# Seven-product MLPs: the order of block sums, evictions and splits, and the place of the token scale

## The chip, the cores and the metric

The kernel runs on one core of one Trainium2 chip. The metric is the device time of one execution in microseconds; one execution was also taken by the hardware profiler, and all rows below are of that one.

## What is computed

Four layers over 512 tokens of 1024 features: sparse attention, a gated convolution, a gated linear recurrence, a gated linear attention. Behind each of the first two stands an MLP, which the change is about:

```python
def rmsnorm(x, g):
    y = xf * lax.rsqrt(jnp.mean(xf * xf, axis=-1, keepdims=True) + EPS)
    return (y * g.astype(jnp.float32)).astype(x.dtype)

def sq_relu_mlp(h, w1, w2):                     # w1 1024x4096, w2 4096x1024
    return jnp.square(jax.nn.relu(h @ w1)) @ w2
...
        h = h + sq_relu_mlp(rmsnorm(h, norm_mlp_g[i]), mlp_w1[i], mlp_w2[i])
    return rmsnorm(h, final_g)                  # then the third layer, which begins with rmsnorm_2
```

## The kernel before, in words

Activations lie features by tokens, `h` as eight tiles of 128x512. Every matrix product is done three times, with both operands split into a rounded high part and a remainder: `whi`, `wlo` for weights, `XH`, `XL` for inputs, `UH`, `UL` for hidden features. Weights come as 512 KB chunks of 128x1024 in one fixed stream (`wall`), issued on SyncE's queue by `dma_to` (L114) into four `stg` buffers, or into named blocks. `split_to` (L121) makes `whi` on ScalarE (L130) and `wlo` on VectorE (L131); both go into a ring of three pairs, and every fourth split of an MLP into a pair of its own (`mine`), for which the splitting runs three items ahead instead of two (`next_weights`). The order on each engine is the order of the code; there is no scheduler.

`chunk` multiplies one weight chunk with eight input tiles: 24 matmuls of 128x512. Outputs take one of three PSUM banks ("mm"), which a later output may use when the earlier one has been read.

`mlp` (from L590) runs eight groups of 512 hidden features. Each of the first seven has a feature stage of four chunks (m = 0 to 3) and a product stage of seven products. A group's part of `h @ w1` goes through relu (L611) and square (L612) on ScalarE into `raw`. The second matrix product is done on halves of tokens and features with seven products in place of eight: the left operands are sums of token halves of `raw` (`left`, L623 and L627 to L629, VectorE; `parts` splits them, L616 on ScalarE and L617 on GpSimd), the right operands are the blocks B11, B21, B22 of `w2` and the sums T3, T2, T4, T1 of blocks (`right`, L638 to L644, VectorE; T1 is written over B12). The products run in the order of `PRODUCTS`: B11, T3, B21, T2, T4, T1, B22. Each has two output tiles of six matmuls (L694 to L696), and but for T1 and B22, which stay in PSUM over all groups, VectorE adds each tile to a sum in SBUF (`sums`, L703; ScalarE copies in the first group, L701). These additions are the evictions spoken of here.

The norm's scale of a token is applied late: relu then square makes it the square of the scale, which is held per token as `cols` and, spread over partitions, as `rs2`. In the seventh group's end the sums are combined (`gather`), scaled by `cols` and transposed back onto `h` (L720, L722). The eighth group is plain: its features `u` are split whole (L671, L672), and eight outputs of 12 matmuls are multiplied by `rs2` (L759) and added to `h` (L760). Behind each output `after` splits `h` for the next layer (`operand`: XH on ScalarE, XL on VectorE, L283) and adds its square to `sacc` (`add_sq`: square on ScalarE, addition on GpSimd, L291). In the second MLP (`halves`) the sum of squares for its own norm is made inside its first group, at m = 1 and 2, and its `after_last` sums squares twice, into `sacc` and, scaled by `final_g`, into `sacc2`. The layer behind it begins with chunks xa0, xa1, xa2 on the unscaled input; `comb_a` turns both sums into scales `rc` and `r2` behind xa1 and `comb_b` spreads them by TensorE behind xa2. `softplus_neg`, 27 small VectorE instructions, is issued between xa0 and xa1.

## Time and profile before

| | us |
|---|---|
| median of 3 runs | 1885.51 (1884.52 to 1885.54) |
| the profiled execution's own time | 1884.3 |
| its span, first to last instruction | 1882.5 |
| TensorE busy | 1780.7 |
| mean granted clock of TensorE | 0.976 |

A granted clock of 1.00 is TensorE's full rate. In a timeline a row gives start, duration, engine, line, instruction and, in brackets, the idle time ahead of it and what ended it; "x2" merges two neighbours. The rows come below.

### The profile page before, as it was taken

Reading aid. Unit: us, or ns where it says so; the run is one execution under the profiler, and the core shown is the slowest. Engines: PE = TensorE matmul, PEld = TensorE weight load, DVE = VectorE, ACT = ScalarE, POOL = GpSimd, SP = SyncE. Lnnn points to the kernel's source line nnn. Section 1 sums busy time; section 2 is a strip of 40 time slices with the busy share of each in tenths; the row PEclk is TensorE's granted clock in tenths of the full one; section 3 lists DMA queues with packets and bytes.
Section 4 is the critical chain, followed back from the end, with each engine's and each line's share of the span. In section 5 each row is a group of like instructions: output and inputs, shape, how many; then the busy total and the mean of one; then the engine's idle time right before and its main releaser. Section 6 shows DMA issues by size and latency. Waiting matters only on the chain.

```text
span 1882.5 us, 22829 instructions
## 1 busy us (share of the span) xinstructions
PE 1780.7 (95%) x8712; PEld 1482.2 (79%) x8712; DVE 1214.9 (65%) x1688; ACT 934.0 (50%) x1424; POOL 503.9 (27%) x408
## 2 busy tenths in 40 slices
PE   9999999988898999898988898989999999999998
PEld 7887787777777778897777777778888788988887
DVE  5896455666667757756666676697676753565354
ACT  5334545444344534556444444557766654356553
POOL 1433311211112202436121112151231200662230
PEclk9999999999999999999999999999999999999999
DMA  5221114322221123103322231222222232232121
GB/s 184 79 90 57 57 63 150 101 90 89 79 101 45 57 88 112 45 24 124 101 79 79 93 98 55 82 97 81 99 95 85 90 101 90 90 107 68 52 72 46
DMA packets 45934, 159.71 MB, mean 85 GB/s; under 512 B 5217, under 2 KB 6625, under 8 KB 45824
## 3 DMA queue, kind: packets, MB, share of 16 engines
q1 hardware_dynamic: 45824, 158.24, 25.4%
q8 instruction: 69, 1.13, 0.2%
q14 instruction: 41, 0.34, 0.1%
HBM read 156.13 MB, written 2.10 MB: 84 GB/s over the span
## 4 chain that ended last, share of the span: by engine, by line
PE 73%; DVE 14%; ACT 7%; issue 5%; POOL 1%; DMA 0%; SPq 0%; DVEq 0%; ACTq 0%; POOLq 0%
PE w L177 4%; PE w L178 4%; PE w L176 4%; DVE wlo L131 3%; PE w L694 3%; PE w L695 3%; PE w L696 3%; ACT whi L130 2%; PE ko L177 1%; PE ko L176 1%; PE ko L178 1%; PE a L176 1%; PE a L177 1%; PE a L178 1%; DVE raw L629 1%
## 5 line engine op out<-in xcount | busy, mean ns | idle before, releaser
L131 DVE TENSOR_TENSOR wlo<-stg,whi 128x1024 fp32r<-128x1024 f32 x191 | 248.4, 1305 | 139.4 <-ACT whi L130 138.1
L130 ACT ACTIVATE whi<-stg 128x1024 fp32r<-128x1024 f32 x228 | 239.1, 1053 | 148.8 <-PE w L695 40.5
L617 POOL TENSOR_TENSOR UL<-raw,UH 128x512 fp32r<-128x512 f32 (+1 forms) x84 | 130.9, 1558 | 475.9 <-ACT UH L616 430.2
L176 PE MATMUL w<-XH,whi 128*128 128x512 f32 (+1 forms) x520 | 202.2, 389 | 0.0
L178 PE MATMUL w<-XH,wlo 128*128 128x512 f32 (+1 forms) x520 | 201.6, 388 | 0.0
L177 PE MATMUL w<-XL,whi 128*128 128x512 f32 (+1 forms) x520 | 201.4, 387 | 0.0
L694 PE MATMUL w<-whi,UH 128*128 128x512 f32 x280 | 120.5, 430 | 54.7 <-DVE sB L703 47.2
L695 PE MATMUL w<-whi,UL 128*128 128x512 f32 x280 | 117.1, 418 | 4.4 <-POOL UL L617 4.4
L131 POOL TENSOR_TENSOR wlo<-stg,whi 128x1024 fp32r<-128x1024 f32 x37 | 89.2, 2417 | 109.9 <-ACT whi L130 109.8
L694 PEld LDWEIGHTS w<-whi,UH 128*128 128x128 f32 x280 | 57.4, 205 | 75.2 <-DVE sB L703 52.4
L696 PE MATMUL w<-wlo,UH 128*128 128x512 f32 x280 | 116.3, 415 | 0.0
L291 POOL TENSOR_TENSOR sacc<-sacc,sq 128x512 f32<-128x512 f32 (+1 forms) x57 | 75.4, 1331 | 147.0 <-ACT sq L290 82.9
L178 PEld LDWEIGHTS w<-XH,wlo 128*128 128x128 f32 x520 | 97.7, 188 | 20.6
L177 PEld LDWEIGHTS w<-XL,whi 128*128 128x128 f32 x520 | 97.7, 188 | 20.3
L176 PEld LDWEIGHTS w<-XH,whi 128*128 128x128 f32 x520 | 97.7, 188 | 20.1
L611 ACT ACTIVATE relu<-w 128x512 f32<-128x512 f32 x64 | 38.1, 595 | 140.8 <-PE w L178 139.8
L616 ACT ACTIVATE UH<-raw 128x512 fp32r<-128x512 f32 (+1 forms) x84 | 59.1, 704 | 81.2 <-DVE raw L629 60.5
L131 DVE TENSOR_TENSOR wlo<-B,whi 128x1024 fp32r<-128x1024 f32 x56 | 76.3, 1365 | 27.1 <-ACT whi L130 27.1
L130 ACT ACTIVATE whi<-B 128x1024 fp32r<-128x1024 f32 x56 | 58.9, 1052 | 68.8 <-PE w L695 68.8
L176 PE MATMUL ko<-XH,whi 128*128 128x256 f32 x256 | 75.5, 295 | 2.4 <-ACT XH L977 2.4
L177 PE MATMUL ko<-XL,whi 128*128 128x256 f32 x256 | 74.5, 291 | 2.3 <-DVE XL L979 1.6
L178 PE MATMUL ko<-XH,wlo 128*128 128x256 f32 x256 | 74.1, 290 | 0.0
(528 smaller groups left out, 4860.7 us busy)
## 6 DMA issues: line engine op xcount, KB each, us to landing
stg<-wall SPq DMA_DIRECT2D x228, 512.0 KB, 3.3
B<-wall SPq DMA_DIRECT2D x56, 512.0 KB, 3.5
gst<-gwall SPq DMA_DIRECT2D x4, 512.0 KB, 3.8
h<-xT SPq DMA_DIRECT2D x3, 512.0 KB, 5.9
out<-yo SPq DMA_DIRECT2D x6, 256.0 KB, 2.5
stg<-wall SPq DMA_DIRECT2D x8, 128.0 KB, 4.8
h<-xT SPq DMA_DIRECT2D x2, 256.0 KB, 3.9
ex<-wglr SPq DMA_DIRECT2D x2, 256.0 KB, 2.7
```

What stands on the lines that cost most here:

```text
L130: act.activation(hi, src, AF.Copy)
L131: eng.tensor_tensor(out=lo, in0=src, in1=hi, op=ALU.subtract)
L176: pe.matmul(o, lhsT=hi[:, w], rhs=xh[:, k, ns], start=first, stop=False)
L177: pe.matmul(o, lhsT=hi[:, w], rhs=xl[:, k, ns], start=False, stop=False)
L178: pe.matmul(o, lhsT=lo[:, w], rhs=xh[:, k, ns], start=False, stop=last)
L291: eng.tensor_tensor(out=acc, in0=acc, in1=t, op=ALU.add)
L611: act.activation(r, o, AF.Relu)
L616: act.activation(UH[:, j, u0:u1, :], raw[:, r0:r1, :], AF.Copy)
L617: pool.tensor_tensor(out=UL[:, j, u0:u1, :], in0=raw[:, r0:r1, :], in1=UH[:, j, u0:u1, :], op=ALU.subtract)
L694: pe.matmul(o, lhsT=UH[:, j, i, xs], rhs=hi[:, js], start=s0, stop=False)
L695: pe.matmul(o, lhsT=UL[:, j, i, xs], rhs=hi[:, js], start=False, stop=False)
L696: pe.matmul(o, lhsT=UH[:, j, i, xs], rhs=lo[:, js], start=False, stop=s1)
```

## The change

Four things. In the groups, each sum of weight blocks is issued one chunk earlier, and the last three left parts (4 to 6 of the second half) are split behind the first product's evictions rather than in the feature stage; splits that run three items ahead are issued behind a product's evictions rather than ahead of its matmuls. In the plain group the token scale is multiplied into `u` and no longer into the outputs, and the transposes of `gather` come one chunk later. In the second MLP, the additions of squares for its norm go from GpSimd to VectorE, two a chunk. And the scaled sum of squares `sacc2` is made on VectorE behind xa0 instead of on GpSimd in `after_last`.

```diff
 # left
-                    parts(j, raw, 4, 7, 5)
+                    if j == 0:
+                        parts(j, raw, 4, 7, 5)
 # right
                 if m == 0:
                     for n in ("T2", "T3", "T4"):
                         f[n] = mp.tile([P, 1024], F32, tag=n, name=n, bufs=1)
+                    dve.tensor_tensor(out=f["T3"], in0=f["B22"], in1=f["B12"], op=ALU.subtract)
                 elif m == 1:
-                    dve.tensor_tensor(out=f["T3"], in0=f["B22"], in1=f["B12"], op=ALU.subtract)
-                elif m == 2:
                     dve.tensor_tensor(out=f["T2"], in0=f["T3"], in1=f["B11"], op=ALU.add)
                     dve.tensor_tensor(out=f["T4"], in0=f["T2"], in1=f["B21"], op=ALU.subtract)
-                else:
+                elif m == 2:
                     f["T1"] = f["B12"]
                     dve.tensor_tensor(out=f["T1"], in0=f["B12"], in1=f["B11"], op=ALU.subtract)
 # groups
-                    if halves and g == 0 and m in (1, 2):
-                        for q in range(4 * m - 4, 4 * m):
-                            add_sq(q, h[:, q, :], sacc)
+                    if halves and g == 0:
+                        for q in (2 * m, 2 * m + 1):
+                            add_sq(q, h[:, q, :], sacc, eng=dve)
...
                         hidden(m, o, u.rearrange("p (a b) -> p a b", a=2))
+                        dve.tensor_tensor(out=u, in0=u, in1=rs2, op=ALU.mult)
...
-                for n, i in PRODUCTS:
-                    hi, lo = next_weights()
+                for p, (n, i) in enumerate(PRODUCTS):
+                    hi, lo = weights(2)
...
                             dve.tensor_tensor(out=a, in0=o, in1=a, op=ALU.add)
+                    if p == 0:
+                        parts(1, raw, 4, 7, 5)
+                    if any(mine(cur[0] + q) for q in range(3)):
+                        split_to(cur[0] + 2)
 # gather
+                        elif m == 2:
                             back("T4", 1, 0)
-                        elif m == 2:
                             back("T3", 1, 4)
+                        else:
                             back("T2", 0, 4)
-                        else:
                             back("B11", 0, 0)
 # outputs of the plain group
-                t = tmp("y")
-                dve.tensor_tensor(out=t, in0=o, in1=rs2, op=ALU.mult)
-                dve.tensor_tensor(out=h[:, m, :], in0=h[:, m, :], in1=t, op=ALU.add)
+                dve.tensor_tensor(out=h[:, m, :], in0=o, in1=h[:, m, :], op=ALU.add)
 # after_last
-        add_sq(m, h[:, m, :], sacc2, scale=V("gfin", m))
 # do_xa, behind the matmuls of xa0
             if m == 0:
+                for q in range(KD):
+                    add_sq(q, h[:, q, :], sacc2, scale=V("gfin", q), eng=dve)
                 softplus_neg()
```

VectorE, third group of the first MLP, end of the feature stage and first evictions (sB11, sT3 are the sums, the numbers are buffers), before:

```order
L131 TENSOR_TENSOR wlo_3246<-B21_2997,whi_3245 128x1024
L627 TENSOR_TENSOR raw_3235<-raw_3235 128x256
L628 TENSOR_TENSOR raw_3235<-raw_3235 128x256
L629 TENSOR_TENSOR raw_3235<-raw_3235 128x256
L644 TENSOR_TENSOR B12_3043<-B12_3043,B11_2995 128x1024
L131 TENSOR_TENSOR wlo_3289<-T2_3161,whi_3288 128x1024
L703 TENSOR_TENSOR sB11_2474<-w2_3292,sB11_2474 128x512
L703 TENSOR_TENSOR sB11_2474<-w2_3300,sB11_2474 128x512
L703 TENSOR_TENSOR sT3_2475<-w2_3308,sT3_2475 128x512
L703 TENSOR_TENSOR sT3_2475<-w2_3316,sT3_2475 128x512
```

The same place now:

```order
L644 TENSOR_TENSOR B12_3059<-B12_3059,B11_2995 128x1024
L131 TENSOR_TENSOR wlo_3247<-B21_2997,whi_3246 128x1024
L627 TENSOR_TENSOR raw_3237<-raw_3237 128x256
L628 TENSOR_TENSOR raw_3237<-raw_3237 128x256
L629 TENSOR_TENSOR raw_3237<-raw_3237 128x256
L704 TENSOR_TENSOR sB11_2474<-w2_3282,sB11_2474 128x512
L704 TENSOR_TENSOR sB11_2474<-w2_3290,sB11_2474 128x512
L131 TENSOR_TENSOR wlo_3305<-T2_3161,whi_3304 128x1024
L704 TENSOR_TENSOR sT3_2475<-w2_3308,sT3_2475 128x512
L704 TENSOR_TENSOR sT3_2475<-w2_3316,sT3_2475 128x512
```

The sum T1 (written to B12) went from behind the three feature sums to ahead of the split, and the split of T2 from ahead of the evictions of sB11 to behind them.

VectorE behind the second MLP, from the last XL of the next layer's input to the first steps of `softplus_neg` (de, s1); before:

```order
L283 SCALAR_TENSOR_TENSOR XL_79<-h_77,gfe_6903,XH_78 128x512 x2
L131 TENSOR_TENSOR wlo_9564<-stg_9376,whi_9563 128x1024
L1071 TENSOR_SCALAR de_9595<-ex_9593 128x16
L1072 RECIPROCAL de_9595<-de_9595 128x16
L1074 TENSOR_TENSOR s1_9598<-ex_9593,de_9595 128x16
```

The same place now:

```order
L283 SCALAR_TENSOR_TENSOR XL_79<-h_77,gfe_6891,XH_78 128x512 x2
L131 TENSOR_TENSOR wlo_9518<-stg_9363,whi_9517 128x1024
L291 TENSOR_TENSOR sacc2_122<-sacc2_122,sq_9546 128x512
L291 TENSOR_TENSOR sacc2_122<-sacc2_122,sq_9549 128x512
L291 TENSOR_TENSOR sacc2_122<-sacc2_122,sq_9552 128x512
L291 TENSOR_TENSOR sacc2_122<-sacc2_122,sq_9555 128x512
L291 TENSOR_TENSOR sacc2_122<-sacc2_122,sq_9558 128x512
L291 TENSOR_TENSOR sacc2_122<-sacc2_122,sq_9561 128x512
L291 TENSOR_TENSOR sacc2_122<-sacc2_122,sq_9564 128x512
L1073 TENSOR_SCALAR de_9571<-ex_9569 128x16
L1074 RECIPROCAL de_9571<-de_9571 128x16
```

Seven additions into sacc2 came in between the split of a chunk and the first step of softplus.

## Rows read from the trace of the kernel before

**Rows 1.** The page: busy time, share of the span, instructions of each engine.

```profile
PE 1780.7 (95%) x8712; PEld 1482.2 (79%) x8712; DVE 1214.9 (65%) x1688; ACT 934.0 (50%) x1424; POOL 503.9 (27%) x408
```

**Rows 2.** TensorE's waits, whole span: releaser: us in total, times, longest.

```profile
PE w L694 <- DVE sB L703: 47.2, 12, 5.5
PE xa L177 <- DVE XL L283: 5.9, 2, 3.5
PE w L695 <- POOL UL L617: 4.4, 1, 4.4
PE w L694 <- DVE sT L703: 3.6, 4, 0.9
PE a L177 <- DVE XL L283: 3.1, 3, 2.0
...
PE w L694 <- ACT sB L701: 2.9, 1, 2.9
```

**Rows 3.** Timeline of TensorE's matmuls, first MLP, third group: start, duration in us.

```profile
392.05 0.39 PE L695 MATMUL w<-whi,UL 128*128 128x512 f32 x1
392.28 0.39 PE L696 MATMUL w<-wlo,UH 128*128 128x512 f32 x1
398.14 0.80 PE L694 MATMUL w<-whi,UH 128*128 128x512 f32 x1 [5.47 <-DVE sB L703]
...
403.42 0.50 PE L694 MATMUL w<-whi,UH 128*128 128x512 f32 x1
```

**Rows 4.** Stretches: busy us by engine (instructions), granted clock, DMA share, GB/s.

```profile
304.20:314.20 10.00, 9.99 (x36) 8.00 (x37) 4.09 (x4) 6.38 (x10) 0.00 (x0) 0.83 0.38 127
350.00:360.00 10.00, 9.09 (x38) 7.16 (x39) 9.39 (x12) 4.19 (x5) 1.06 (x1) 1.00 0.57 187
...
398.00:403.00 5.00, 4.86 (x12) 3.81 (x12) 3.17 (x6) 1.06 (x1) 0.00 (x0) 0.50 0.21 84
...
658.60:668.60 10.00, 7.23 (x26) 5.30 (x26) 6.94 (x6) 5.07 (x7) 3.53 (x7) 0.83 0.49 142
...
1242.00:1252.00 10.00, 7.57 (x21) 5.30 (x22) 8.86 (x16) 4.67 (x8) 5.84 (x4) 0.66 0.27 74
```

**Rows 5.** Timeline of VectorE, the same group.

```profile
387.89 2.20 DVE L641 TENSOR_TENSOR T<-T,B 128x1024 f32<-128x1024 f32 x1
390.02 1.21 DVE L131 TENSOR_TENSOR wlo<-B,whi 128x1024 fp32r<-128x1024 f32 x1
391.15 1.51 DVE L627 TENSOR_TENSOR raw<-raw 128x256 f32<-128x256 f32 x1
...
395.44 2.04 DVE L131 TENSOR_TENSOR wlo<-T,whi 128x1024 fp32r<-128x1024 f32 x1 [0.72 <-ACT whi L130]
397.40 1.27 DVE L703 TENSOR_TENSOR sB<-w,sB 128x512 f32<-128x512 f32 x2
```

**Rows 6.** Timeline of ScalarE and of GpSimd, the same group.

```profile
388.56 0.60 ACT L611 ACTIVATE relu<-w 128x512 f32<-128x512 f32 x1 [0.23 <-PE w L178]
...
394.59 1.81 POOL L617 TENSOR_TENSOR UL<-raw,UH 128x768 fp32r<-128x768 f32 x1 [2.21 <-issue]
```

**Rows 7.** Timeline of GpSimd and VectorE, the group ahead of it.

```profile
349.23 1.83 POOL L617 TENSOR_TENSOR UL<-raw,UH 128x768 fp32r<-128x768 f32 x1 [1.29 <-issue]
...
349.28 1.27 DVE L703 TENSOR_TENSOR sB<-w,sB 128x512 f32<-128x512 f32 x2
```

**Rows 8.** Timeline of GpSimd, second MLP, first group.

```profile
870.88 7.29 POOL L291 TENSOR_TENSOR sacc<-sacc,sq 128x512 f32<-128x512 f32 x4
```

**Rows 9.** Timeline of VectorE, plain group of the first MLP.

```profile
657.16 0.69 DVE L760 TENSOR_TENSOR h<-h,y 128x512 f32<-128x512 f32 x1
```

**Rows 10.** Timeline of VectorE, then of TensorE, behind the second MLP.

```profile
1250.01 0.18 DVE L1071 TENSOR_SCALAR de<-ex 128x16 f32<-128x16 f32 x1 [0.80 <-ACT ex L1069]
...
1260.31 0.16 DVE L1098 TENSOR_TENSOR r<-r,rc 128x4 f32<-128x4 f32 x1
...
1261.81 0.60 PE L303 MATMUL spread<-ident,r 128*128 128x128 f32 x4
```

## The prediction

> **What bounds the kernel now.** The page comes first: TensorE is busy 95% of the span and no other engine over 65% [rows 1], so the time is TensorE's own work plus whatever makes it wait or run slowly. Second the table of TensorE's waits [rows 2]: almost all of its idle time lies in the two MLPs, and one row leads: 47.2 us in twelve waits for a VectorE eviction of a product sum (sB). Six rows that this change touches come to 47.2 + 5.9 + 4.4 + 3.6 + 3.1 + 2.9 = 67.1 us. Third the timeline of one such wait [rows 3]: a 128x512 matmul follows the next after 0.23 us ahead of it, then comes a gap of 5.47 us, and from 398.14 to 403.42 there are twelve steps of 0.44 us. The granted clock of that stretch is 0.50 [rows 4], the 1.2 GHz level in place of 2.4, so a long wait is paid twice. Fourth the granted clock in the ten microseconds from the end of each wait [rows 4]: 1.00 after waits of about 1.3 us, 0.83 after one of 2.9 us, 0.66 at the worst place. Twelve such windows lose clock (first and last shown), together 27.3 us; I take 27, since a little of it lies in idle time counted already. The ceiling for this change is 67.1 + 27 = 94.1 us.
>
> **Where the long wait comes from.** It is one of order. The matmul output has three banks, so with the third tile of products done (392.5) TensorE needs the first eviction. VectorE reaches it at 397.40 [rows 5], because ahead of it in its queue stand, from 387.89 on: sum T4 (2.20), a split (1.21), three feature sums (1.51 and two of 0.42), sum T1 (1.21, the split's form) and the split of T2 (2.04). The 0.42 is what is left: 391.15 to the idle time ahead of 395.44 are 3.57, less 1.51 and 1.21, for two. Two of these are long only because VectorE stood behind GpSimd: a split takes 1.21 at 390.02 and 2.04 at 395.44, where GpSimd's 1.81 us subtraction began first [rows 5, 6].
>
> **Sums one chunk earlier, evictions ahead of splits.** No instruction is added here; T3, T2/T4 and T1 move to the chunk before, and the last three feature parts (ScalarE copy, GpSimd subtraction) and the split of T2 go behind the first product's two evictions. In the trace's group of 388 us the new queue reads so: T4 is done in the chunk before (VectorE is idle there; cover exists, one chunk is 24 x 0.23 = 5.5 us). Ahead of the eviction remain T1 1.21, one split 1.2 to 1.7, three feature sums 0.42 + 0.42 + 0.42 plus up to 1.0 for one GpSimd overlap. The feature sums can't start before ScalarE's relu and square, 388.56 + 0.6 + 0.6 = 389.8 [rows 6]. So the eviction starts between 391.1 (389.8 and three sums, nothing in the way) and 393.3 (all of it in the way), and frees its bank 0.75 later: TensorE waits between 0 and 1.5 us in place of 5.47. What is late next is the seventh tile, whose bank waits for the evictions of T3, and ahead of those VectorE now meets the moved split of T2, which waits for the moved GpSimd subtraction (1.81): about 1.0 more. I added the row durations queue by queue in this way for every group, with VectorE and GpSimd excluding each other where both read two SBUF tiles. Done on the old order, the six waits of one MLP for sB come to 24.3 us where the trace has 47.2 / 2 = 23.6, and that is my warrant for it. On the new order it leaves 1.4, 2.4, 1.5, 1.5, 1.5 and 2.4 us in the six groups behind the first, no single wait over 1.5. In the first group, whose evictions are ScalarE's, the 2.9 us wait goes. That is 10.7 us left per MLP, 21.4 in both. SP's queue: block loads are issued when the sum T1 or a split has read the old block; in the new order that is earlier or up to one product (2.8 us) later, while a block is next read a chunk or more after it lands.
>
> The Trainium skill, "SBUF — State Buffer", "Who interferes with whom", says that a VectorE instruction with two SBUF inputs and a GpSimd instruction that reads SBUF exclude each other for the whole instruction. This speaks against moving the subtraction to where the T2 split meets it. The trace agrees (2.04 against 1.21); had they merely shared bandwidth, the second wait of a group would be about 0.7 us shorter, some 8 us in all. The same section exempts an instruction with one SBUF input, and the evictions beside a GpSimd subtraction [rows 7], 1.27 for two, show that.
>
> **Squares of the second MLP's input to VectorE.** Seven GpSimd additions leave its queue in the first group, four of them in one run of 7.29 us [rows 8], behind which a feature part came late; the 4.4 us wait goes. VectorE gets seven of 0.69 [rows 9], two a chunk, beside 5.5 us of matmuls. My walk leaves 1.0 us at the first product's UL. Bounds 0 and 2.
>
> **Token scale into the last group's features.** At the end one of two VectorE instructions per output goes (about 0.7), the addition stays. Four multiplications (0.69, by the two-tile addition of [rows 9]) go in ahead of the feature copies, three hidden by 5.5 us chunks; the fourth delays the last feature part by 0.7, but the transposes that the gather now issues there (eight more) keep TensorE busy for 0.9, so nothing is added; uncovered it would be 0.7 per MLP. At the end VectorE's pair of outputs sinks by 1.4 us; the first chunk behind MLP 1 loses its 3.1 us waits and their slow matmuls, the first behind MLP 2 its 5.9 us, where GpSimd also loses eight additions. The gather moves transposes by one chunk; its own 1.5 us wait stays.
>
> **The second sum of squares, moved behind chunk xa0.** Here something is given back. Eight ScalarE squares and seven VectorE additions (0.69 by [rows 9], each needing the last: about 5.0) now stand ahead of the softplus chain and of the scale r. From the first step of that chain to r are 10.5 us in the trace (1250.01 to 1260.47), and r is done 1.3 us before TensorE asks for it with its transposes at 1261.81 [rows 10]. VectorE can begin the additions 4.5 us behind the start of xa0, when its last XL and a split are out, so they end at 9.6 and r comes at 20.1; TensorE, which no longer stalls in xa0, asks after three chunks and the means, 3 x 5.46 + 1.6 = 18.0. Bounds: 0, if softplus isn't blocked by GpSimd as it was in the trace, and 5, if the additions are; my walk has 2.0, and 1.4 for slow matmuls behind it. I take 3.4.
>
> **Sum.** 94.1 - 21.4 (groups) - 1.0 (first group) - 3.4 (r) - 1.5 (a slow matmul, 0.1, behind each small wait) = 66.8 us. The profiled execution took 1884.3 (span 1882.5, 1.8 around it): 1817.5. The median of the runs shown, 1885.5, is 1.2 higher, so I forecast 1819.
>
> **Rivals.** *Small waits hold the clock down.* A group has two or three waits of 0.4 to 1.5 us in 8 us. For it: behind three waits of 3.1 us together at the end of MLP 1 the clock fell to 0.83 [rows 4]. Against: two waits in a group of 350 us left 1.00 [rows 4]. If every one of the twelve groups loses 1.7 us (0.83 of 10 us), 20 us go: 1839. The Trainium skill, "TensorE: Matmul & The Clock Gate", "A second HAM failure mode: psum-queue depth-cycling", describes this: frequent micro-idles between matmul groups while output banks cycle make the clock oscillate. The waits after 350 us speak against it here, the sum of several for it.
>
> *The small waits vanish*, if the feature sums miss GpSimd each time: 22 us less, 1797.
>
> *The order reaches only half.* The eviction still stands behind the three feature sums; were these blocked by GpSimd twice, it comes at 395 and a 2.5 to 3 us wait with its 1.7 us of clock stays: 12 x 4.5 - 21 = 33 us more, 1852.
>
> *Slower: splits late.* VectorE now does two evictions (1.27) and then a split (1.21) for each product, 2.5 us against 12 x 0.23 = 2.76 of matmuls. If a product took VectorE over 2.76, TensorE would wait for a wlo at every one of 98 products; it eats up the whole gain of 67 when a product takes 0.7 more than that. With the split blocked as at 395.44 (2.04) and an eviction held up by half a microsecond in each product it would be 3.8: 98 x 1.0 - 67 = 31 us more than now, 1916. Against: GpSimd works in one product of seven.
>
> *Nothing changes*: if another wait of equal length stood behind the eviction. The queue lists show none.
>
> **How the numbers follow.** Forecast 0.60 (1806 to 1830 for errors of 0.5 us in each group's wait); clock held down 0.15 (1839); small waits vanish 0.10 (1797); half 0.07 (1852); slower 0.05; no change 0.03. The range 1800 to 1840 holds the first two and half of the third, 0.80. Faster by over 0.2% 0.92, within 0.2% 0.03, slower 0.05; 0.2% (3.8 us) is about what a measurement of this kernel can tell from no change.
>
> **What would show it.** Right: the sB row under 25 us and none over 1.6; no wait for UL or XL over 1.5 us; granted clock of the ten microseconds behind each group's waits near 1.00; a new wait of about 2 us of "spread" for r. Wrong: sB waits near 3 us; windows at 0.8 with short waits; wlo as a releaser of TensorE.

## The result, and the profile after

The changed kernel takes 1825.09 us (median of four runs, 1824.04 to 1827.32) against 1885.34: a ratio of 0.9683, 95% interval 0.9666 to 0.9700, or 60.3 us less. The forecast was 1819. The profiled execution has a span of 1825.6, at the upper end of its runs.

The page's line of busy times, which answers to [rows 1]:

```profile
PE 1764.9 (97%) x8712; PEld 1469.5 (80%) x8712; DVE 1205.7 (66%) x1694; ACT 932.4 (51%) x1424; POOL 480.3 (26%) x394
```

TensorE's waits over the whole span (line waited on, releaser, us in total, times, longest), which answer to [rows 2]:

```profile
PE w L695 <- DVE sT L704: 9.0, 10, 0.9
PE w L695 <- DVE sB L704: 5.6, 10, 1.4
PE w L696 <- POOL UL L617: 4.9, 6, 1.1
...
PE w L695 <- ACT UH L616: 3.4, 1, 3.4
PE yT L725 <- DVE sT L714: 2.6, 2, 1.3
...
PE spread L303 <- DVE r L1100: 2.0, 1, 2.0
```

The row of 47.2 us has become one of 5.6, and no wait in it is over 1.4. The waits for XL behind both MLPs are gone. Four things stand in the place: many short waits for sT and UL, one of 3.4 us for UH, and one of 2.0 for the scale r. The third group of the first MLP, TensorE and then VectorE, answers to [rows 3, 5]:

```profile
389.65 0.39 PE L697 MATMUL w<-wlo,UH 128*128 128x512 f32 x1
390.46 0.50 PE L695 MATMUL w<-whi,UH 128*128 128x512 f32 x1 [0.42 <-DVE sB L704]
...
394.41 0.50 PE L695 MATMUL w<-whi,UH 128*128 128x512 f32 x1 [0.90 <-DVE sT L704]
394.74 0.39 PE L696 MATMUL w<-whi,UL 128*128 128x512 f32 x1
394.97 0.40 PE L697 MATMUL w<-wlo,UH 128*128 128x512 f32 x1
```

```profile
387.48 0.41 DVE L627 TENSOR_TENSOR raw<-raw 128x256 f32<-128x256 f32 x1
387.93 1.42 DVE L628 TENSOR_TENSOR raw<-raw 128x256 f32<-128x256 f32 x1
389.38 0.42 DVE L629 TENSOR_TENSOR raw<-raw 128x256 f32<-128x256 f32 x1
389.72 1.28 DVE L704 TENSOR_TENSOR sB<-w,sB 128x512 f32<-128x512 f32 x2
391.66 2.09 DVE L131 TENSOR_TENSOR wlo<-T,whi 128x1024 fp32r<-128x1024 f32 x1 [0.66 <-ACT whi L130]
393.68 1.27 DVE L704 TENSOR_TENSOR sT<-w,sT 128x512 f32<-128x512 f32 x2
```

The eviction of sB now stands directly behind the feature sums, and TensorE waits 0.42 us for it in place of 5.47. The split of T2, which stood ahead of it, has become the next thing that is late: 2.09 us, with a wait of 0.90 behind it. Behind neither wait does the pace fall: steps of 0.23 us go on. The granted clock (the third number from the end, columns as in [rows 4]) of stretches with such waits, of the stretch behind the wait of 3.4 us, and of the one behind the wait of 2.0:

```profile
347.00:357.00 10.00, 9.06 (x40) 7.11 (x39) 9.47 (x11) 4.52 (x5) 1.54 (x1) 1.00 0.17 53
387.00:397.00 10.00, 8.68 (x37) 6.46 (x36) 9.27 (x12) 5.38 (x6) 3.14 (x2) 1.00 0.27 96
477.00:487.00 10.00, 9.63 (x42) 7.73 (x43) 10.00 (x13) 4.54 (x5) 1.42 (x1) 1.00 0.31 104
849.90:859.90 10.00, 9.11 (x29) 6.99 (x30) 8.10 (x8) 8.45 (x15) 4.87 (x3) 0.70 0.34 107
1203.00:1213.00 10.00, 9.85 (x41) 8.20 (x42) 9.09 (x13) 4.68 (x8) 0.00 (x0) 0.83 0.43 150
```

The waits of 0.25 to 1.39 us in the groups leave the full clock; the two longer ones do not. Length alone does not decide it: in ul_vector and t3_back (below) the same wait of 2.0 us for r leaves 1.00.

Lengths on TensorE, taken as differences of starts in the timelines (the seven groups of the first MLP, its plain group's features, its eight outputs; then the same for the second MLP's first group alone), in us:

| kernel | g1 | g2 | g3 | g4 | g5 | g6 | g7 | features | outputs | 2nd MLP g1 |
|---|---|---|---|---|---|---|---|---|---|---|
| before | 45.9 | 45.4 | 49.4 | 48.3 | 48.4 | 44.1 | 48.3 | 27.0 | 22.3 | 49.6 |
| changed | 42.8 | 44.3 | 44.1 | 42.8 | 42.9 | 43.0 | 44.1 | 26.9 | 22.4 | 48.5 |
| undo_sums | 41.5 | 44.2 | 44.2 | 43.4 | 47.8 | 43.0 | 45.8 | 26.9 | 22.4 | 46.6 |
| undo_parts | 44.1 | 44.2 | 44.1 | 42.8 | 48.2 | 43.0 | 44.1 | 26.9 | 22.4 | 48.7 |
| undo_splits | 42.4 | 45.4 | 44.1 | 42.8 | 45.6 | 44.1 | 44.0 | 26.9 | 22.4 | 47.9 |
| order_only | 42.7 | 44.3 | 44.1 | 42.8 | 42.9 | 43.0 | 44.1 | 25.4 | 21.6 | 51.3 |
| undo_scale | 42.5 | 44.3 | 44.1 | 42.8 | 42.9 | 43.0 | 44.1 | 25.4 | 21.6 | 47.4 |
| ul_vector | 44.8 | 43.1 | 43.0 | 41.7 | 42.9 | 41.8 | 43.0 | 26.9 | 22.4 | 47.6 |
| t3_back | 43.2 | 44.2 | 44.1 | 42.8 | 42.9 | 43.0 | 44.1 | 26.9 | 22.4 | 43.9 |

The first groups differ by up to 2.6 us also between kernels that are alike there (in the first MLP 42.2 to 44.8 for ul_vector, all_three and three_edits; in the second 47.4 to 49.9 for the changed kernel, undo_scale, undo_sacc2 and softplus_late); the others repeat to 0.1 us. By stage, before to changed: first MLP 379.1 to 353.4, the convolution behind it 197.2 to 194.4, second MLP 383.0 to 359.1, from there to the spread of r 27.3 to 20.5, from there to the first matmul of gc 66.5 to 68.2, the rest unchanged. The sum is 57 us in these two executions.

### The profile page after: what moved, and what is told of

It reads as the page before. It is cut to its first block, busy times and chain, and to the rows that moved or that the text cites. A ratio compares the mean times of both kernels' runs of the same rounds, so it can differ in the third digit from the quotient of the medians.

```text
span 1825.6 us, 22775 instructions
## 1 busy us (share of the span) xinstructions
PE 1764.9 (97%) x8712; PEld 1469.5 (80%) x8712; DVE 1205.7 (66%) x1694; ACT 932.4 (51%) x1424; POOL 480.3 (26%) x394
## 3 DMA queue, kind: packets, MB, share of 16 engines
q1 hardware_dynamic: 45824, 158.24, 25.8%
## 4 chain that ended last, share of the span: by engine, by line
PE 71%; DVE 15%; ACT 7%; issue 5%; DMA 1%; POOL 1%; SPq 0%; DVEq 0%; ACTq 0%; POOLq 0%
PE w L177 4%; PE w L178 4%; PE w L176 4%; DVE wlo L131 4%; PE w L695 2%; PE w L696 2%; PE w L697 2%; ACT whi L130 2%; PE ko L177 1%; PE ko L176 1%; PE ko L178 1%; PE a L176 1%; PE a L178 1%; PE a L177 1%; PE lg L499 1%
## 5 line engine op out<-in xcount | busy, mean ns | idle before, releaser
L131 DVE TENSOR_TENSOR wlo<-stg,whi 128x1024 fp32r<-128x1024 f32 x191 | 242.5, 1279 | 124.8 <-ACT whi L130 124.4
L695 PE MATMUL w<-whi,UH 128*128 128x512 f32 x280 | 113.7, 406 | 18.3 <-DVE sT L704 9.0
L696 PE MATMUL w<-whi,UL 128*128 128x512 f32 x280 | 111.2, 397 | 4.9 <-POOL UL L617 4.9
L177 PEld LDWEIGHTS w<-XL,whi 128*128 128x128 f32 x520 | 97.7, 188 | 20.5
L697 PE MATMUL w<-wlo,UH 128*128 128x512 f32 x280 | 110.4, 394 | 0.0
L291 POOL TENSOR_TENSOR sacc<-sacc,sq 128x512 f32<-128x512 f32 (+1 forms) x43 | 49.1, 1145 | 146.5 <-ACT sq L290 82.9
L695 PEld LDWEIGHTS w<-whi,UH 128*128 128x128 f32 x280 | 53.0, 189 | 39.7 <-DVE sT L704 13.7
L131 DVE TENSOR_TENSOR wlo<-B,whi 128x1024 fp32r<-128x1024 f32 x56 | 75.0, 1339 | 12.3 <-ACT whi L130 12.3
```

Source lines behind the costliest of these rows:

```text
L131: eng.tensor_tensor(out=lo, in0=src, in1=hi, op=ALU.subtract)
L177: pe.matmul(o, lhsT=hi[:, w], rhs=xl[:, k, ns], start=False, stop=False)
L291: eng.tensor_tensor(out=acc, in0=acc, in1=t, op=ALU.add)
L695: pe.matmul(o, lhsT=UH[:, j, i, xs], rhs=hi[:, js], start=s0, stop=False)
L696: pe.matmul(o, lhsT=UL[:, j, i, xs], rhs=hi[:, js], start=False, stop=False)
L697: pe.matmul(o, lhsT=UH[:, j, i, xs], rhs=lo[:, js], start=False, stop=s1)
```

## The experiments

| kernel | median (lowest to highest) | ratio to before, 95% interval |
|---|---|---|
| changed | 1825.1 (1824.0 to 1827.3) | 0.9683 (0.9666 to 0.9700) |
| order_only | 1832.9 (1832.3 to 1834.1) | 0.9728 (0.9714 to 0.9741) |
| undo_sums | 1839.1 (1836.9 to 1840.2) | 0.9759 (0.9745 to 0.9774) |
| undo_parts | 1835.6 (1832.6 to 1838.1) | 0.9742 (0.9726 to 0.9757) |
| undo_splits | 1834.0 (1833.5 to 1835.1) | 0.9735 (0.9719 to 0.9751) |
| undo_scale | 1830.4 (1827.8 to 1831.8) | 0.9711 (0.9698 to 0.9724) |
| undo_sacc2 | 1826.3 (1826.0 to 1830.9) | 0.9697 (0.9684 to 0.9710) |
| softplus_late | 1822.2 (1821.0 to 1824.2) | 0.9671 (0.9658 to 0.9684) |
| t3_back | 1819.2 (1818.7 to 1820.3) | 0.9655 (0.9642 to 0.9668) |
| t3_back_sq_gpsimd | 1826.1 (1825.1 to 1828.3) | 0.9692 (0.9678 to 0.9705) |
| ul_vector | 1811.4 (1809.7 to 1813.7) | 0.9614 (0.9600 to 0.9627) |
| all_three | 1811.9 (1810.2 to 1813.5) | 0.9616 (0.9602 to 0.9631) |
| three_edits | 1807.8 (1806.8 to 1810.8) | 0.9596 (0.9582 to 0.9609) |

**The order alone.** The kernel before with the new order of sums, parts, splits and transposes, and nothing else; against the changed kernel:

```diff
 # token scale
-                        dve.tensor_tensor(out=u, in0=u, in1=rs2, op=ALU.mult)
...
-                dve.tensor_tensor(out=h[:, m, :], in0=o, in1=h[:, m, :], op=ALU.add)
+                t = tmp("y")
+                dve.tensor_tensor(out=t, in0=o, in1=rs2, op=ALU.mult)
+                dve.tensor_tensor(out=h[:, m, :], in0=h[:, m, :], in1=t, op=ALU.add)
 # squares of the second MLP's input
-                    if halves and g == 0:
-                        for q in (2 * m, 2 * m + 1):
-                            add_sq(q, h[:, q, :], sacc, eng=dve)
+                    if halves and g == 0 and m in (1, 2):
+                        for q in range(4 * m - 4, 4 * m):
+                            add_sq(q, h[:, q, :], sacc)
 # second sum of squares
+        add_sq(m, h[:, m, :], sacc2, scale=V("gfin", m))
...
-                for q in range(KD):
-                    add_sq(q, h[:, q, :], sacc2, scale=V("gfin", q), eng=dve)
```

> Of the change only the order of sums, evictions, splits and transposes; token scale at the outputs, squares of the second MLP on GpSimd and the second sum of squares in after_last as in the kernel before. Theory (the order in the groups carries most of it): adding up the queues gives 17 us more than the whole change, 1842; sB waits as in the changed kernel (under 8 us), the waits for UL (about 4) in the second MLP and for XL behind both MLPs (about 9 in sum) as before. Rival (the waits in the groups go only together with the lighter VectorE of the other parts): sB waits over 15 us in sum, over 1855.

It takes 1832.9: 51.8 us less than the kernel before, which took 1884.6 in the runs beside it; the whole change is worth 60.3. Its row of waits for sB:

```profile
PE w L694 <- DVE sB L703: 5.5, 10, 1.4
```

Its groups two to seven are those of the changed kernel to a tenth, so the rival falls. The other three parts together are worth 7.8 us, where adding up the queues had said 17: the estimate for them was too high. Inside the plain group this kernel is the faster one (25.4 and 21.6 against 26.9 and 22.4), which the token scale has to answer for.

**Each move of the order undone.**

```diff
 # undo_sums
-                    dve.tensor_tensor(out=f["T3"], in0=f["B22"], in1=f["B12"], op=ALU.subtract)
                 elif m == 1:
+                    dve.tensor_tensor(out=f["T3"], in0=f["B22"], in1=f["B12"], op=ALU.subtract)
+                elif m == 2:
                     dve.tensor_tensor(out=f["T2"], in0=f["T3"], in1=f["B11"], op=ALU.add)
...
-                elif m == 2:
+                else:
                     f["T1"] = f["B12"]
 # undo_parts
-                    if j == 0:
-                        parts(j, raw, 4, 7, 5)
+                    parts(j, raw, 4, 7, 5)
...
-                    if p == 0:
-                        parts(1, raw, 4, 7, 5)
 # undo_splits
-                    hi, lo = weights(2)
+                    hi, lo = next_weights()
...
-                    if any(mine(cur[0] + q) for q in range(3)):
-                        split_to(cur[0] + 2)
```

> Changed kernel, but T3, T2 and T4, and T1 are issued in chunks 1, 2 and 3 again; the rest stays. Theory (three pieces of VectorE work stood ahead of a group's first eviction, and each piece moved away counts by its own length): T1 and part of T4 stand ahead of it again, waits for sB of 2.0 to 4.3 us in most groups, 20 us more: 1845. Rival 1 (any one of the moves alone is enough): under 5 us more, 1826 to 1830. Rival 2 (only all moves together bring anything): sB waits near 47 us again, 1865 or more.

> Changed kernel, but the last three left parts of the second half are split in the feature stage again, ahead of the first product; the rest stays. Theory (as for the sums): ScalarE's copy and GpSimd's subtraction then come in front of the split of T2; in the groups where a four-apart split falls on that place the wait for sB is 4.2 us, elsewhere 0.4 to 1.1 us; 16 us more: 1841. Rival 1 (this move is only worth what it takes from one engine's queue): under 5 us more. Rival 2 (all moves are needed): 1865 or more.

> Changed kernel, but splits that run three items ahead are issued ahead of a product's matmuls again; the rest stays. Theory (as for the sums): the split of T2 (1.2 to 2.0 us) stands ahead of the first evictions in some of the groups, waits for sB of 1.6 to 4.3 us, 20 us more: 1845. Rival 1: under 5 us more. Rival 2 (all moves are needed): 1865 or more.

They cost 14.0, 10.5 and 8.9 us, so neither rival holds: no one move is enough, and none is needed for the rest to work. The queue sums (20, 16, 20) have the places right and the sizes 1.4 to 2.2 times too large. The sB row of each (total, times, longest):

```profile
PE w L696 <- DVE sB L705: 28.4, 12, 4.2
```

```profile
PE w L694 <- DVE sB L703: 11.0, 10, 4.1
```

```profile
PE w L695 <- DVE sB L704: 14.6, 10, 2.5
```

The table of groups tells what each is for. With the sums back the fourth, fifth and seventh group of the first MLP lose 0.6, 4.9 and 1.7 us, and there is no row for sT any more: the late eviction has taken its place. With the parts back, what stands clear of the spread falls on the fifth group of each MLP (48.2 and, in the second, 47.2, against 42.9): there the split ahead of the evictions is one of the four-apart ones, and it waits for ScalarE, whose copy of the parts came first. The first group's 44.1 against 42.8 is within what first groups differ by. VectorE in the fifth group of undo_parts:

```profile
478.41 2.03 DVE L131 TENSOR_TENSOR wlo<-B,whi 128x1024 fp32r<-128x1024 f32 x1 [1.86 <-ACT whi L130]
480.37 1.27 DVE L703 TENSOR_TENSOR sB<-w,sB 128x512 f32<-128x512 f32 x2
```

1.86 us of idle VectorE and a split of 2.03 stand ahead of the eviction. The three costs add up to 33.4 us. The order's 51.8 also holds the later transposes, 2.3 us in each MLP (see the token scale below), which leaves about 47: undone singly the three moves cost less than they bring together, so here a move that is made last pays less than one that is made first.

**The wait for UH in the second MLP's first group.** VectorE there, in the changed kernel:

```profile
830.96 0.43 DVE L623 TENSOR_TENSOR raw<-raw 128x256 f32<-128x256 f32 x1 [0.17 <-ACT raw L612]
836.34 1.23 DVE L638 TENSOR_TENSOR T<-B,B 128x1024 f32<-128x1024 f32 x1 [4.96 <-DMA B<-wall]
837.49 2.32 DVE L131 TENSOR_TENSOR wlo<-B,whi 128x1024 fp32r<-128x1024 f32 x1
...
849.98 0.80 PE L695 MATMUL w<-whi,UH 128*128 128x512 f32 x1 [3.40 <-ACT UH L616]
```

The last row is TensorE's. T3, moved to chunk 0, stands for 4.96 us because block B22, asked for some 5 us into the MLP, has not landed, and everything behind it in VectorE's queue stands with it. Kernel t3_back moves T3 of this one group behind chunk 1's feature sums:

```diff
...
-                    dve.tensor_tensor(out=f["T3"], in0=f["B22"], in1=f["B12"], op=ALU.subtract)
+                    if not (halves and g == 0):
+                        dve.tensor_tensor(out=f["T3"], in0=f["B22"], in1=f["B12"], op=ALU.subtract)
                 elif m == 1:
+                    if halves and g == 0:
+                        dve.tensor_tensor(out=f["T3"], in0=f["B22"], in1=f["B12"], op=ALU.subtract)
```

> The changed kernel takes 1825.1; in the second MLP's first group TensorE waits 3.4 us for UH and 0.8 for UL, and then runs at a granted clock of 0.66 for ten microseconds. Here T3 of that one group is issued behind chunk 1's feature sums, as in the kernel before; all else stays. Theory A (the sum T3 waits 4.96 us on VectorE for the load of its block, and the whole queue behind it is late): the UH wait falls under 1.5 us, the clock comes back, 3 to 6 us less: 1819 to 1822. Rival B (the seven additions of squares that VectorE got make it late): the UH wait stays over 2.5 us and the time within 1.5 us of 1825. Adding up the queues with the landing time put in gives a middle: UH wait 0.8, UL wait 1.3, 1 to 4 us less.

1819.2, 5.9 us less. The wait for UH and the clock of the ten microseconds behind it:

```profile
843.76 0.49 PE L698 MATMUL w<-whi,UH 128*128 128x512 f32 x1 [0.71 <-ACT UH L616]
```

```profile
843.70:853.70 10.00, 8.84 (x37) 7.00 (x38) 9.01 (x9) 9.50 (x17) 4.91 (x3) 1.00 0.31 107
```

Theory A holds: the wait falls from 3.40 to 0.71, the clock from 849.9 on had been 0.70 and is 1.00, and the group takes 43.9 in place of 48.5 us, well under the 47.4 to 49.9 of the kernels alike there. That is 4.6 of the 5.9 us. The two profiles differ by another 3.2 us in the convolution, which the edit does not touch, so the group's figure is the surer one. The squares are not the cause of the 3.4 us; they are the next question. Kernel t3_back_sq_gpsimd is t3_back with the squares as in order_only:

> As t3_back (1819.2), but the squares of the second MLP's input are added on GpSimd in chunks 1 and 2 again. Theory (GpSimd's additions hold up a feature part, as the 4.4 us wait for UL of the kernel before): a wait for UL of 3 to 4.5 us in that MLP's first product, slow matmuls behind it, 5 to 6 us more: 1824 to 1825. Rival (with the order changed GpSimd has time, and VectorE is the late one): UH wait of 0.7 goes, 1817 to 1819.

With the squares back on GpSimd the time is 1826.1, 6.9 more, a little over what the theory gave, and by two waits in place of one: 3.9 us for UH and 1.9 for UL. GpSimd's run of four additions, and VectorE beside it:

```profile
840.11 8.03 POOL L291 TENSOR_TENSOR sacc<-sacc,sq 128x512 f32<-128x512 f32 x4
```

```profile
843.32 2.29 DVE L131 TENSOR_TENSOR wlo<-T,whi 128x1024 fp32r<-128x1024 f32 x1
845.53 1.48 DVE L623 TENSOR_TENSOR raw<-raw 128x256 f32<-128x256 f32 x1
```

Each of these VectorE instructions takes 1.1 us longer than it does elsewhere (0.42 becomes 1.48, 1.22 becomes 2.29). So moving the squares is worth 6.9 us, once T3 no longer hides it; the group alone takes 50.8 us against 43.9.

**The waits for sT.** The moved subtraction on VectorE, behind T3's evictions:

```diff
...
-                    if p == 0:
-                        parts(1, raw, 4, 7, 5)
+                    if p == 1:
+                        parts(1, raw, 4, 7, 5, eng=dve)
```

> Changed kernel, but the moved subtraction (UL of parts 4 to 6) is VectorE's, issued with its copy behind the evictions of T3. Theory (the ten waits for sT, 9.0 us, come from the split of T2 that stands still while GpSimd subtracts, 2.09 us against 1.21): the split takes 1.2, the sT row goes under 1.5 us, 11 us less: 1814. Rival (that split is late for its high part from ScalarE, 0.66 us of idle time ahead of it, and GpSimd does not matter): sT waits stay over 5 us in sum, and VectorE's extra 0.9 us per group adds up to 5 us: 1824 to 1830.

1811.4, 13.7 us less. The same place as above:

```profile
391.97 1.28 DVE L704 TENSOR_TENSOR sB<-w,sB 128x512 f32<-128x512 f32 x2
393.17 1.21 DVE L131 TENSOR_TENSOR wlo<-T,whi 128x1024 fp32r<-128x1024 f32 x1
394.31 1.28 DVE L704 TENSOR_TENSOR sT<-w,sT 128x512 f32<-128x512 f32 x2
395.50 0.95 DVE L617 TENSOR_TENSOR UL<-raw,UH 128x768 fp32r<-128x768 f32 x1
```

The split takes 1.21 us, no wait for sT is left in the groups, and groups two to four, six and seven are 1.1 to 1.2 us shorter each; the fifth, which had no such wait, is not. In the two MLPs that is 10.4 us (353.4 to 349.7 and 359.1 to 352.4), close to the 11 expected. Another 3.2 of the difference between the two profiles lies in the convolution, which the edit does not touch.

But the edit changes two things at once. `parts` is a copy on ScalarE and a subtraction, and both moved one product later. ScalarE in the changed kernel, then in ul_vector:

```profile
389.84 0.85 ACT L616 ACTIVATE UH<-raw 128x768 fp32r<-128x768 f32 x1 [2.20 <-DVE raw L629]
390.59 1.99 ACT L130 ACTIVATE whi<-T 128x1024 fp32r<-128x1024 f32 x2
```

```profile
389.77 1.05 ACT L130 ACTIVATE whi<-T 128x1024 fp32r<-128x1024 f32 x1
```

In the changed kernel the copy stands ahead of the high part of T2, and the split idles 0.66 us for it; in ul_vector the high part is made first and the split does not wait. So ul_vector takes away the 0.66 us of the rival together with the 0.88 us that the split loses beside GpSimd (2.09 against 1.21). Which of the two sets the wait of 0.90 is not shown: a kernel with the subtraction behind T3's evictions but still on GpSimd was not run.

The Trainium skill, "SBUF — State Buffer", "Who interferes with whom", has it that a VectorE instruction with two SBUF inputs and a GpSimd instruction that reads SBUF exclude each other. The trace agrees: the split takes 2.09 us beside GpSimd's 1.86 us subtraction and 1.21 without it. VectorE's own subtraction takes 0.95.

**The token scale.** Multiplied into the outputs again, as in order_only, the rest as changed.

> Changed kernel, but the token scale is multiplied into the outputs again, two VectorE instructions each; transposes and the second sum of squares stay as changed. With order alone changed, the plain group took 25.4 us and its outputs 21.6, against 26.9 and 22.4 in the changed kernel, so inside the MLPs 4.6 us go. Theory A (behind the MLPs the scale in the features is worth more than that): the waits for XL behind the first MLP return with their slow matmuls, 5.5 us, and behind the second about half of the 5.2 us and its slow matmuls, 3 to 5 us: 1829 to 1831. Rival B (behind the second MLP the waits for XL came from GpSimd's eight additions into the second sum, not from the second instruction per output): 1826. Rival C (the scale in the features brings nothing): 1821.

1830.4, by theory A: waits for XL come back behind both MLPs, 2.4 us each. The scale in the features costs 2.3 us in each MLP (features 26.9 against 25.4, outputs 22.4 against 21.6) and gives back more behind them: the convolution takes 197.4 us without it and 194.4 with it, and to the spread of r it is 25.8 and 20.5. The cost inside is mostly two waits. With the order alone the transposes of the gather, one chunk later, wait for nothing, and neither do the outputs; with the multiplication on VectorE's queue the transposes wait 1.30 us and the outputs 0.47 us for UL. VectorE, then TensorE, there in the changed kernel:

```profile
596.85 0.69 DVE L671 TENSOR_TENSOR u<-u,rs 128x512 f32<-128x512 f32 x1
597.46 1.28 DVE L714 TENSOR_TENSOR sT<-keepB,sT 128x512 f32<-128x512 f32 x2
598.65 2.12 DVE L714 TENSOR_TENSOR sB<-sB,sB 128x512 f32<-128x512 f32 x2
...
598.20 1.53 PE L725 MATMUL yT<-ident,sT 128*128 128x128 f32 x12 [1.30 <-DVE sT L714]
```

**The second sum of squares.** Made in after_last on GpSimd again, as in order_only, the rest as changed.

> Changed kernel, but the second sum of squares is made in after_last on GpSimd again. The wait for r (2.0 us and slow matmuls behind it, about 3.8) goes. Theory A (GpSimd's eight additions stand in the way of XL behind the second MLP): a wait for XL of 3 to 5 us in the first chunk behind it and slow matmuls, in all 3.4 us more than the changed kernel: 1828 to 1829. Rival B (those waits came from the second VectorE instruction per output, which stays away here): no wait for XL over 1 us, 1821.

1826.3, which can't be told from 1825.1. Theory A misses, and rival B has the waits right and the time wrong: no wait for XL comes back, but the wait for r does not go, it grows to 4.2 us. Set beside each other, the waits for XL behind the second MLP (5.9 us before, 5.2 in order_only, 2.4 in undo_scale, none in undo_sacc2) come from the second VectorE instruction per output; GpSimd's additions alone bring none, but lengthen the waits where that instruction is there. GpSimd's queue, then ScalarE's and VectorE's first steps of softplus, in undo_sacc2:

```profile
1176.46 15.55 POOL L291 TENSOR_TENSOR sacc<-sacc,sq 128x512 f32<-128x512 f32 x9
```

```profile
1192.05 0.22 ACT L1070 ACTIVATE al<-vec 128x16 f32<-128x16 f32 x1 [4.76 <-POOL sacc L291]
```

```profile
1193.90 0.17 DVE L1074 TENSOR_SCALAR de<-ex 128x16 f32<-128x16 f32 x1 [4.29 <-ACT ex L1072]
```

GpSimd adds until 1192.0, softplus begins only then, and r stands behind softplus. Counted from the last matmul of the second MLP, softplus begins on VectorE after 12.3 us here and after 10.2 in the changed kernel, and r is done after 22.6 and 20.4; in the kernel before it was 26.0. So the additions make r late on either engine, least on VectorE; what stands between them and r is softplus itself. Kernel softplus_late:

```diff
-                softplus_neg()
                 gate_split()
...
             if m == 1:
                 comb_a()
+                softplus_neg()
```

> Changed kernel, but the 27 small instructions of softplus are issued behind comb_a instead of ahead of it. Theory (the scale r is late by 2.0 us because the seven additions into sacc2 came ahead of softplus, which stands ahead of r): the wait of spread for r goes, with the slow matmuls behind it 3 to 4 us less: 1821 to 1822. Rival (softplus now delays the split or the multiplication of xa behind it, or r waits for its mean anyway): a wait of 1 us or more for a split, for xa or for the softplus result instead, 1824 to 1827.

1822.2, 2.9 us less. The mean and r, in softplus_late:

```profile
1193.53 1.05 PE L298 MATMUL mean<-onesc,sacc 128*128 128x1 f32 x8 [0.30 <-DVE sacc L291]
1200.01 0.60 PE L303 MATMUL spread<-ident,r 128*128 128x128 f32 x4
```

No wait for r is left, and r's spread comes 1.7 us sooner (18.8 against 20.5). Part of it comes back 30 us later, where the chunk za waits 0.8 and 0.2 us for its input.

**Together.** Both kernels have the edits of t3_back, ul_vector and softplus_late; all_three has this as well:

```diff
-                    if halves and g == 0:
-                        for q in (2 * m, 2 * m + 1):
+                    if halves and g == 0 and m == 0:
+                        for q in range(KD):
```

> Changed kernel with three edits together: T3 of the second MLP's first group behind chunk 1's feature sums, the moved subtraction on VectorE behind T3's evictions, softplus behind comb_a; also all eight squares of the second MLP's input behind its chunk 0. Alone they took 5.9, 13.7 and 2.9 us off. Theory (three separate places): they add up, 1825.1 - 22.5 = 1802.6, with no wait for UH over 1 us, none for sT or for r. Rival (what one frees another takes, since all three load VectorE): 1806 to 1811.4, the best of the three.

> The three edits as in all_three, but the squares stay two a chunk as in the changed kernel. In all_three (1811.9) the second MLP's first product still waited 2.2 us for UH, against 0.7 with T3 moved back alone, so the eight squares behind chunk 0 are taken to have made it late. Theory (the three edits are separate and add up): 1825.1 - 5.9 - 13.7 - 2.9 = 1802.6, UH wait under 1 us. Rival (the edits share VectorE, the gain of one is used up by another): 1807 or more.

1811.9 and 1807.8. The kernels differ in the place of the eight squares alone. Behind chunk 0 they bring back a UH wait of 2.2 us (0.7 in three_edits), but the group is only 1.6 us longer for it (47.0 against 45.4). Another 2.0 of the 4.1 us lie behind the second MLP, where the clock of all_three is 0.83 in the ten microseconds behind a wait of 0.65 us for the mean, and 1.00 in three_edits behind one of 0.29. That the squares cause this part is not shown. three_edits is the fastest kernel of this study, 17.3 us under the changed one. That is 5 us short of the expected 22.5, and by the number the rival was right, but its mechanism finds no row: groups two to seven and the features are those of ul_vector to a tenth. Only the second MLP's first group is longer than in t3_back, 45.4 against 43.9, and the waits there are the same two (0.71 for UH, 1.1 for UL); the clock behind them is 0.83 instead of 1.00. The parts in the MLPs and ahead of r add up to 16.4 (10.4, 4.3 from 353.4 to 353.8 and 359.1 to 354.4, and 1.7 from 20.5 to 18.8); the medians of t3_back and ul_vector held more than their stages, 3.2 us of each profile's difference lying in the convolution.

## Why the prediction was right, and where it was not

- **What bounds the kernel, and where the long wait comes from: right.** Undoing each of the three moves brings a part of the sB row back, in groups that the queues name. The order alone gives 51.8 us.
- **The size left in the groups: right.** In the changed kernel there are ten waits for sT, ten for sB and the four of 0.75 for UL; in the first MLP's groups two to seven they come to 8.8 us by the rows, against 10.7 forecast, and the longest is 1.39 against 1.5. The second wait of a group was forecast from the split of T2 standing beside the moved subtraction, and the rows have it (2.09 us). The 0.66 us that the same split waits for ScalarE's copy are not named in the forecast, and ul_vector, which takes both away (10.4 us inside the MLPs), cannot say how much is exclusion.
- **Squares to VectorE: the term was mis-sized, and this is most of the miss.** The wait that the term forecast comes from the sum T3, moved ahead, and not from the squares. The step said 1.0 us for the first product's UL, bounds 0 and 2, and the step on the order that a block "is next read a chunk or more after it lands". In the second MLP's first group all four blocks and four chunks are asked for within 5 us, B22 lands 12.9 us into the MLP, and T3, moved ahead to chunk 0, is read before that. The wait was 3.4 + 0.8 us, with the clock at 0.70 for the ten microseconds behind it, which costs some 3 us more. t3_back takes 4.6 us of this away inside the group.
- **Token scale: right in sum, wrong in its reason.** "Nothing is added" holds: 27.0 and 22.3 us before, 26.9 and 22.4 after. But it is two effects that cancel: the later transposes save 2.3 us in each MLP (order_only) and the multiplication costs them again. The wait of the gather went by the order and came back with the multiplication. The scale pays behind the MLPs; net of its cost inside them it is worth 5.3 us by the medians.
- **Second sum of squares: right in size, half right in its cause.** A wait of 2.0 us for r was forecast and stands there, by the forecast's own path: the additions, then softplus, then r. But the move is not what costs it. Undone, the wait is 4.2 us, since softplus then begins later still, behind GpSimd's additions; and against the kernel before, r comes 5.6 us sooner (20.4 against 26.0). It was early in [rows 10] only because TensorE was held up by XL and came later still, 27.3 us behind the MLP where it now asks after 18.5.
- **The rivals.** *Small waits hold the clock down* does not happen in the groups of the changed kernel: 1.00 with three waits of 0.4 to 0.9 us. The Trainium skill's rule on depth-cycling ("TensorE: Matmul & The Clock Gate", "A second HAM failure mode: psum-queue depth-cycling"), under which it would, is not borne out by these groups. Elsewhere single short waits were followed by less (0.65 us by 0.83 in all_three), at no such price as the rival's 20 us. *Half* and *slower* find no row: no product waited for a wlo in the changed kernel. *The small waits vanish* is what ul_vector reaches for, by another edit.
- **The signs.** The sB row, the clock in the groups (but for the second MLP's first) and the new wait for r are as the prediction said they would be. The sign on XL fails once, far from the change: TensorE waits 1.9 us for one at 1575.9, and this wait is 0.4 or 1.9 us in kernels that are alike there. The 3.4 us for UH are in no sign.
- **The sum.** 1819 against 1825.1 is a miss of 6 us. That t3_back then measures 1819.2 is in part luck: the group explains 4.6 of its 5.9 us, groups two to seven of both MLPs wait 17.6 us where 21.4 were forecast, and the convolution differs by 3 us for reasons not known. What else was off (queue sums for single moves too large by 6 to 11 us, the other parts worth 7.8 and not 17) did not enter the forecast of the whole.

**Open.** The convolution took 191.2 to 194.4 us in kernels that are alike there. TensorE waits 2.0 us for u there in both t3_back and the changed kernel, and behind it matmuls follow each other slowly for longer in the changed one (a granted clock of 0.66 over ten microseconds, against 1.00). What decides it was not tried.

## What to carry to other kernels

When several instructions stand ahead of a late one in an in-order queue, list them all: each move pays by what it takes out, here the first more than the last, and the next wait is found behind the instruction that was put back. Before an instruction is moved ahead, look at the earliest time its data are there in the first round of a loop, when all the loads are in flight together, and not only in the steady state. A long wait hides others: when it goes, what was "early" (here r) may turn out to have been early only against an engine that was stalled.

## What the runs showed of the hardware that was not expected

- Small VectorE instructions are held as long as large ones beside GpSimd. In the changed kernel a 128x16 multiplication of softplus, which takes 0.18 us, took 2.26 at 1193.76, beside GpSimd's 2.38 us split:

```profile
1193.61 2.38 POOL L1116 TENSOR_TENSOR gwl<-gst,gwh 128x1024 fp32r<-128x1024 f32 x1 [7.16 <-ACT gwh L1115]
```

```profile
1193.76 2.26 DVE L1082 TENSOR_TENSOR pl<-pl,s 128x16 f32<-128x16 f32 x1
...
1196.33 0.18 DVE L1082 TENSOR_TENSOR pl<-pl,s 128x16 f32<-128x16 f32 x1
```

- Eight 512 KB loads asked for within 5 us land late: in the second MLP's first group the four blocks took 6.4 us (median from issue to landing) and the four chunks behind them 8.8, where a block takes 3.3 (median) over the whole span:

```profile
B<-wall SPq DMA_DIRECT2D x4, 512.0 KB, 6.4
stg<-wall SPq DMA_DIRECT2D x4, 512.0 KB, 8.8
```

- The clock behind a short wait is not settled by the wait's length. The pair of 0.71 and 1.1 us in the second MLP's first group was followed by 1.00 in t3_back and 0.83 in three_edits (ten microseconds each); the wait of 2.0 us for r by 0.83 in the changed kernel and 1.00 in ul_vector and t3_back. No run here shows what decides it. Ten microseconds at 0.83 instead of 1.00 are 1.7 us, so a difference of that size between two single executions says little.
